# Products of 512 token columns issued as two products of 256 columns in one accumulation group

## The chip, the cores and the metric

The kernel runs on one core of a Trainium2 chip. The metric is device time in microseconds (us) for one execution of the whole program. TensorE (PE in the profile) multiplies, VectorE (DVE) and ScalarE (ACT) do the elementwise work and empty the accumulators, GpSimd (POOL) does a little elementwise work, and SyncE (SP) issues the transfers.

## The reference, cut to what matters

A two-layer backbone runs over 512 tokens: 256 context tokens, which form a prefix, and 256 latent tokens. The same weights serve both kinds.

```python
for layer in range(DEPTH):                       # 2 layers
    h_l = modulate(rmsnorm(lat, ...), ...)       # latent tokens
    h_c = modulate(rmsnorm(cx, ...), ...)        # context tokens
    ...
    if layer % 2 == 0:                           # layer 0: SSD + retention heads
        y_c, st = ssd_retention_mixer(h_c, None, ab_zero_states(b), *p)
        y_l, _ = ssd_retention_mixer(h_l, rope, st, *p)
    else:                                        # layer 1: mLSTM heads
        ...
    lat = block_update(lat, y_l, ...)            # residual, then the feed-forward network
    if layer < DEPTH - 1:
        cx = block_update(cx, y_c, ...)

def swiglu(h, w1, w3, w2):
    return (jax.nn.silu(h @ w1) * (h @ w3)) @ w2
```

Nearly all arithmetic is in the dense products: the input projection `ab_in_w` (1024 x 6160), the output projection `ab_out_w` (2048 x 1024), two feed-forward networks with 2816 hidden columns, and the mLSTM's `ml_up_w` (1024 x 4096) and `ml_down_w` (2048 x 1024). Everything is float32, and the kernel keeps that accuracy by splitting each operand into two parts (below).

## The kernel before, in words

**Layout.** Activations lie feature by token: 128 features on the partitions, tokens along the free dimension. Columns 0 to 255 are the context (`CT_`), columns 256 to 511 the latent tokens (`LT_`). So a product of one weight tile (128 x 128, stationary, loaded by a LDWEIGHTS before each matmul) with all tokens streams 512 columns and fills one accumulator tile of 128 x 512 float32, one bank of the accumulator memory.

**Split products.** Weights arrive as float32 (`wraw`), and ACT rounds each to fp32r (`wH`, L367) while DVE takes what is left (`wL`, L227). Activations are split the same way (`hH`, `hL` for the normalised input, `uH`, `uL` for the hidden layer of the feed-forward network, `yH`, `yL` for what enters the output projection). The helper `mm3` (L401 to L407) then issues three matmuls for each pair of a weight tile and an activation tile, wH with H, wH with L, wL with H, and adds them all up in one accumulation group. L405, L406 and L407 are these three. Every such matmul has a LDWEIGHTS of its own (PEld in the profile).

**Who calls `mm3` with how many columns.** With 512 columns: the four query and key tiles of the very first stage (`p4`, L591), the input projection's feature tiles (`projA`, L698), the output projection (`out_quarter`, L1038), and layer 0's feed-forward network (`ffn0`, L1144), which takes `projA` for its first product and its own loop for the second. With 256 columns: `projB` (L705), in which an activation tile is stationary and 256 weight columns stream; the last four output tiles before each norm (`tail_tiles`, L1002); the first tiles after it (`head_tiles`, L1022), which work on one half of a 512-column accumulator at a time; and all of layer 1, whose `projA` already works half by half (L701), since its activations are stored in halves (`packed`).

**Feed-forward network of layer 0.** The 22 hidden tiles come in three parts of 8, 8 and 6. In each part `projA` makes two tiles, `ffn_act` (L1131) turns them into one hidden tile (ACT: silu, DVE: `u`, ACT: `uH`, DVE: `uL`), and when all tiles of the part are there, the second product (called f2 here, L1162) accumulates over them, hidden tile after hidden tile, and DVE adds the result to the residual stream (`upd`, L974).

**Order.** A scheduler that is part of the framework orders the instructions of PE, ACT, DVE and POOL; SP's order is the program's. PE executes its matmuls in the order given, and one that waits for an operand holds up all behind it. There are four accumulator tiles for these products (`mmps`, tag "mm") and four buffers each for `wH` and `wL`.

Of the kernel before, what the change touches and what calls it, by code (L numbers as in the profile page):

```python
# [186 lines left out]
def tile_hybrid(ctx, tc, A, out, dbg=None):  # L187
# [16 lines left out]
    def s2(p="s2", shape=(P, 512), dt=F32):  # L204
        return sb.tile(list(shape), dt, tag="s2", name=nm(p), bufs=36)
# [25 lines left out]
    CT_, LT_, ALL = slice(0, 256), slice(256, 512), slice(0, 512)  # L231
# [169 lines left out]
    def mm3(o, pairs, first=True, last=True):  # L401

        n = len(pairs)
        for i, ((lh, ll), (rh, rl)) in enumerate(pairs):
            TE.matmul(o, lhsT=lh, rhs=rh, start=first and i == 0, stop=False)  # L405
            TE.matmul(o, lhsT=lh, rhs=rl, start=False, stop=False)  # L406
            TE.matmul(o, lhsT=ll, rhs=rh, start=False, stop=last and i == n - 1)  # L407
# [5 lines left out]
    def cols(hl, sl):  # L413
        return tuple(t[:, sl] for t in hl)
# [156 lines left out]
    for i, k in enumerate(seq):  # L571
        ld(i + 3)
        wload()
        if i < 4:
            if i > 0:
                wprep()
            w4.append(wready.pop(0))
        if i == 0:
            xn = h_a(k, rb, amix[0], ALL)
        h_b(hs[k], k, xn, mod[0][0], ALL)  # L580
        if i == 0:
            prep(1)
        prep(i + 2)
        TE.matmul(pdt[0:32, :], lhsT=wdt[:, k, :], rhs=hs[k](ALL)[0], start=i == 0, stop=False)
        TE.matmul(pdt[0:16, :], lhsT=wdt[:, k, 0:16], rhs=hs[k](ALL)[1], start=False, stop=i == KD - 1)
        if i + 1 < KD:
            fin(i + 1)
            xn = h_a(seq[i + 1], rb, amix[0], ALL)
        for j, w in enumerate(w4):
            for n in range(i + 1) if j == i else (i,):  # L590
                mm3(p4[j], [(wk(w, seq[n]), hs[seq[n]](ALL))], n == 0, n == KD - 1)  # L591
# [106 lines left out]
    def projA(hs):  # L698
        w = wnext()
        p = mmps()  # L700
        for sl in (CT_, LT_) if hs[0].packed else (ALL,):  # L701
            mm3(p[:, sl], [(wk(w, k), hs[k](sl)) for k in range(KD)])
        return p

    def projB(hs, evac):  # L705
        ws = [wnext(), wnext()]
        for c in range(NCH):
            p = mmps([P, 256])
            sl = slice(c * P, (c + 1) * P)
            mm3(p, [(hs[k](sl), tuple(ws[k // 4][z][:, (k % 4) * 256:(k % 4 + 1) * 256] for z in range(2)))  # L710
                    for k in range(KD)])
            evac(c, p)
            slot()
# [774 lines left out]
    for m in range(KD):  # L1488
        o = s2("fin")[:, :256]
# [22 lines left out]
```

## Time and profile before

| | |
|---|---|
| time, median of 3 runs | 1348.47 us (1346.25 to 1348.91) |
| the profiled execution, its own time | 1344.61 us |
| its span, from the first to the last instruction | 1342.8 us |
| TensorE busy | 1308.1 us (97%) |
| VectorE busy | 945.6 us (70%) |
| ScalarE busy | 643.2 us (48%) |
| mean granted TensorE clock | 0.988 of full speed |

Matmuls are pipelined: the profile gives each a duration from its start to a modelled end, and these overlap. A 512-column matmul is shown with some 0.39 us, though the next one starts 0.23 us after it. What a matmul costs in a stream is therefore the distance from start to start, and it is read from the times at which instructions start. A TensorE that is shown busy all the time may still stream faster or slower.

### The profile page before, as it was taken

To read this page: it belongs to the slowest core of one execution; us is meant where nothing else is said; L and a number is where in the kernel's file an instruction comes from. 1 tells how busy PE (TensorE), PEld (TensorE's weight loads), DVE (VectorE), ACT (ScalarE), POOL (GpSimd) and SP (SyncE) were. 2 spreads that over 40 slices of the span, in tenths; PEclk is the share of its full clock that TensorE was granted. 3 is DMA by queue.
4 is the path that set the end of the run, shared out by engine and by line. 5 is a ranking of instruction groups with operands and counts; after the bars stand their busy time and mean duration, and the time that the engine had idled before them with its cause. 6 is when DMAs were issued, how large, how long until landed. Compare 5 with 4: busy or idle time off the path is not lost.

```text
span 1342.8 us, 20999 instructions
## 1 busy us (share of the span) xinstructions
PE 1308.1 (97%) x8158; PEld 1147.5 (85%) x8158; DVE 945.6 (70%) x1703; ACT 643.2 (48%) x1114; POOL 124.8 (9%) x138
## 2 busy tenths in 40 slices
PE   7999999999999999999999999989999999999997
PEld 3699888988899898888888888989999689999997
DVE  7888797966865578797557634586666897666555
ACT  4465757836763243222222233466556563544443
POOL 0022032211021030000000210300000000000001
PEclk9999999999999999999999999999999999899998
DMA  9337344434312225566547622411124334365553
GB/s 367 112 144 235 122 163 155 133 117 161 117 64 87 94 79 204 179 213 236 195 170 248 240 94 94 140 66 63 48 69 144 134 109 142 130 206 199 191 196 118
DMA packets 60837, 200.70 MB, mean 149 GB/s; under 512 B 6841, under 2 KB 8377, under 8 KB 60737
## 3 DMA queue, kind: packets, MB, share of 16 engines
q1 hardware_dynamic: 60594, 199.36, 43.0%
q8 instruction: 64, 1.05, 0.3%
q14 instruction: 35, 0.29, 0.1%
q10 hardware_dynamic: 144, 0.01, 0.0%
HBM read 197.16 MB, written 1.13 MB: 148 GB/s over the span
## 4 chain that ended last, share of the span: by engine, by line
PE 82%; DVE 7%; issue 4%; DMA 2%; ACT 2%; POOL 1%; SPq 0%; POOLq 0%; DVEq 0%; ACTq 0%
PE mm L405 24%; PE mm L406 24%; PE mm L407 24%; DVE wL L227 2%; PE sc L954 2%; PE mm L1215 1%; ACT wH L367 1%; PE sc L836 1%; DVE junk L291 1%; DMA ada<-in_ada 1%; DMA wraw<-in_wup 1%; PE sc L841 1%; PE sc L818 1%; DVE junk L267 1%; PE sc L732 1%
## 5 line engine op out<-in xcount | busy, mean ns | idle before, releaser
L367 ACT CAST wH<-wraw 128x1024 fp32r<-128x1024 f32 x248 | 259.4, 1048 | 415.1 <-PE mm L406 298.1
L227 DVE TENSOR_TENSOR wL<-wraw,wH 128x1024 fp32r<-128x1024 f32 x248 | 305.1, 1232 | 139.6 <-ACT wH L367 129.7
L406 PE MATMUL mm<-hL,wH 128*128 128x512 f32 (+1 forms) x568 | 219.7, 387 | 0.4 <-DVE hL L496 0.4
L407 PE MATMUL mm<-hH,wL 128*128 128x512 f32 (+1 forms) x568 | 219.4, 387 | 0.0
L405 PE MATMUL mm<-hH,wH 128*128 128x512 f32 (+1 forms) x568 | 217.7, 390 | 1.5 <-ACT wH L367 1.5
L267 DVE SCALAR_TENSOR_TENSOR junk<-ada,cbc 128x1024 bf16<-128x1024 f32 x128 | 157.9, 1233 | 19.6 <-DMA ada<-in_ada 18.1
L405 PEld LDWEIGHTS mm<-hH,wH 128*128 128x128 f32 x568 | 107.0, 190 | 25.8 <-ACT wH L367 2.0
L406 PEld LDWEIGHTS mm<-hL,wH 128*128 128x128 f32 x568 | 107.7, 190 | 24.4 <-DVE hL L496 0.6
L407 PEld LDWEIGHTS mm<-hH,wL 128*128 128x128 f32 x568 | 107.6, 189 | 23.7
L405 PE MATMUL mm<-wH,hH 128*128 128x256 f32 x384 | 110.4, 288 | 0.0
L979 DVE SCALAR_TENSOR_TENSOR xt<-mm,mod,xt 128x256 f32<-128x256 f32 x144 | 64.4, 479 | 63.8 <-PE mm L407 63.5
L406 PE MATMUL mm<-wL,hH 128*128 128x256 f32 x384 | 107.9, 281 | 0.0
L407 PE MATMUL mm<-wH,hL 128*128 128x256 f32 x384 | 107.4, 280 | 0.0
L405 PE MATMUL mm<-hp,wH 128*128 128x256 f32 x384 | 107.3, 284 | 0.1
L406 PE MATMUL mm<-hp,wH 128*128 128x256 f32 x384 | 106.9, 281 | 0.0
L683 DVE SCALAR_TENSOR_TENSOR conv<-xp,prm,conv 128x512 f32<-128x512 f32 x128 | 96.5, 757 | 14.8 <-ACT conv L680 13.8
L407 PE MATMUL mm<-hp,wL 128*128 128x256 f32 x384 | 106.7, 280 | 0.0
L405 PE MATMUL mm<-hHL,wH 128*128 128x256 f32 x352 | 97.6, 279 | 1.1 <-ACT hHL L495 1.1
L406 PE MATMUL mm<-hHL,wH 128*128 128x256 f32 x352 | 97.7, 278 | 0.0
L407 PE MATMUL mm<-hHL,wL 128*128 128x256 f32 x352 | 97.7, 278 | 0.0
L405 PEld LDWEIGHTS mm<-hp,wH 128*128 128x128 f32 x384 | 72.6, 191 | 2.7 <-ACT conv L680 1.1
L405 PE MATMUL mm<-uH,wH 128*128 128x512 f32 (+1 forms) x200 | 73.6, 368 | 0.0
(329 smaller groups left out, 2876.2 us busy)
## 6 DMA issues: line engine op xcount, KB each, us to landing
wraw<-in_f SPq DMA_DIRECT2D x136, 512.0 KB, 4.0
ada<-in_ada SPq DMA_DIRECT2D x80, 512.0 KB, 4.6
wraw<-in_win SPq DMA_DIRECT2D x48, 512.0 KB, 4.4
wraw<-in_wup SPq DMA_DIRECT2D x32, 512.0 KB, 3.3
erow<-scr SPq DMA_DIRECT2D x16, 512.0 KB, 6.8
wraw<-in_wout SPq DMA_DIRECT2D x16, 512.0 KB, 3.7
wraw<-in_wdn SPq DMA_DIRECT2D x16, 512.0 KB, 3.3
adaf<-in_ada SPq DMA_DIRECT2D x10, 512.0 KB, 8.0
```

Of the source, the lines that this page charges most:

```text
L227: eng.tensor_tensor(out=o, in0=a, in1=b, op=op)
L267: V.scalar_tensor_tensor(out=junk, in0=raw, scalar=1.0, in1=cbc[:, st, :], op0=ALU.mult, op1=ALU.mult, accum_out=mod[l][c][:, k, st:st + 1])
L291: V.scalar_tensor_tensor(out=junk, in0=raw, scalar=1.0, in1=cbc[:, st, :], op0=ALU.mult, op1=ALU.mult, accum_out=to)
L367: S.copy(out=H, in_=raw)
L405: TE.matmul(o, lhsT=lh, rhs=rh, start=first and i == 0, stop=False)
L406: TE.matmul(o, lhsT=lh, rhs=rl, start=False, stop=False)
L407: TE.matmul(o, lhsT=ll, rhs=rh, start=False, stop=last and i == n - 1)
L683: V.scalar_tensor_tensor(out=o, in0=x[:, :, k:k + 256], scalar=pc(wname, t * 5 + k), in1=o, op0=ALU.mult, op1=ALU.add)
L732: TE.transpose(p[:, c * P:(c + 1) * P], tiles[:, c, f * P:(f + 1) * P], ident)
L818: TE.matmul(p[:, d, :], lhsT=btok[:, c, :], rhs=vws[n][:, d, :], start=True, stop=True)
L954: TE.matmul(py[:, i, :], lhsT=src[:, i * P:(i + 1) * P], rhs=vt[:, j, :], start=j == 0, stop=j == len(srcs) - 1)
L979: V.scalar_tensor_tensor(out=xt[:, m, half], in0=p[:, o:o + 256], scalar=gate[:, m, st:st + 1], in1=xt[:, m, half], op0=ALU.mult, op1=ALU.add)
```

## The change

`mm3` looks at the width of its output. Over 256 columns it now calls itself twice, for the context half and then for the latent half of the same accumulator tile. The first call opens the accumulation group, the second closes it. Each of the two goes through all pairs of its list, so that the weight tiles are loaded once more for the second half.

```diff
     def mm3(o, pairs, first=True, last=True):
 
         n = len(pairs)
+        if o.shape[-1] > 256:
+            for sl in (CT_, LT_):
+                mm3(o[:, sl], [(lp, cols(rp, sl)) for lp, rp in pairs], first and sl is CT_, last and sl is LT_)
+            return
         for i, ((lh, ll), (rh, rl)) in enumerate(pairs):
             TE.matmul(o, lhsT=lh, rhs=rh, start=first and i == 0, stop=False)
             TE.matmul(o, lhsT=lh, rhs=rl, start=False, stop=False)
             TE.matmul(o, lhsT=ll, rhs=rh, start=False, stop=last and i == n - 1)
```

The four new lines move the three matmuls to L409, L410 and L411.

Two places on TensorE show what this does to its order. Names are the tiles' with a running number; the halves of a tile are not told apart in them. The first place is in layer 0's feed-forward network, where one `projA` tile ends and the next begins. Before:

```order
L405 MATMUL mm_5109<-hH_4689,wH_4862 128x512
L406 MATMUL mm_5109<-hL_4690,wH_4862 128x512
L407 MATMUL mm_5109<-hH_4689,wL_4863 128x512
L405 MATMUL mm_5159<-hH_4675,wH_5097 128x512
L406 MATMUL mm_5159<-hL_4676,wH_5097 128x512
L407 MATMUL mm_5159<-hH_4675,wL_5098 128x512
```

With the change, inside the second of these tiles (now `mm_6095`), where the context half ends and the latent half begins:

```order
L409 MATMUL mm_6095<-hH_5601,wH_6009 128x256
L410 MATMUL mm_6095<-hL_5602,wH_6009 128x256
L411 MATMUL mm_6095<-hH_5601,wL_6010 128x256
L409 MATMUL mm_6095<-hH_5587,wH_6009 128x256
L410 MATMUL mm_6095<-hL_5588,wH_6009 128x256
L411 MATMUL mm_6095<-hH_5587,wL_6010 128x256
```

The eight activation tiles are gone through twice, with 24 matmuls of 256 columns each time, where there were 24 of 512 columns.

The second place is the start of f2 in the first part of that network, where the last hidden tile (`uH_5624`, `uL_5625` before, `uH_6848`, `uL_6849` with the change) is used for the first time. Before:

```order
L405 MATMUL mm_5649<-uH_5540,wH_5559 128x512
L406 MATMUL mm_5649<-uL_5541,wH_5559 128x512
L407 MATMUL mm_5649<-uH_5540,wL_5560 128x512
L405 MATMUL mm_5649<-uH_5624,wH_5559 128x512
L406 MATMUL mm_5649<-uL_5625,wH_5559 128x512
L407 MATMUL mm_5649<-uH_5624,wL_5560 128x512
```

With the change:

```order
L409 MATMUL mm_6873<-uH_6716,wH_6735 128x256
L410 MATMUL mm_6873<-uL_6717,wH_6735 128x256
L411 MATMUL mm_6873<-uH_6716,wL_6736 128x256
L409 MATMUL mm_6873<-uH_6848,wH_6735 128x256
L409 MATMUL mm_6937<-uH_5999,wH_6790 128x256
L410 MATMUL mm_6937<-uL_6000,wH_6790 128x256
L410 MATMUL mm_6873<-uL_6849,wH_6735 128x256
L411 MATMUL mm_6873<-uH_6848,wL_6736 128x256
L409 MATMUL mm_6873<-uH_5999,wH_6735 128x256
```

Before, 21 matmuls of 512 columns stand between the start of f2 and the first use of the last hidden tile. Now 21 of 256 columns stand there, and the scheduler puts two matmuls of the next output tile (`mm_6937`) between the use of `uH_6848` and that of `uL_6849`, which is thus the 25th matmul of f2. The latent half follows. The second part has the same order. In the third, with six hidden tiles, 16 matmuls and then 8 of the next tile stand ahead of the last `uL`: 24 again. The transfers that SP issues, and POOL's instructions, are the same in the same order; on ACT and DVE some neighbours change places.

## Rows read from the trace of the kernel before

**Rows 1.** The page: span, and busy time, share, and instructions of engines.
```profile
span 1342.8 us, 20999 instructions
...
PE 1308.1 (97%) x8158; PEld 1147.5 (85%) x8158; DVE 945.6 (70%) x1703; ACT 643.2 (48%) x1114; POOL 124.8 (9%) x138
```

**Rows 2.** Busy time in stretches: first tiles; layer 0's mixer; its feed-forward network.
```profile
core 0: us, PE busy (x) PEld busy (x) DVE busy (x) ACT busy (x) POOL busy (x), PEclk, DMA share, GB/s
0.00:60.00 60.00, 49.47 (x176) 28.13 (x177) 50.17 (x129) 22.54 (x43) 1.22 (x5) 0.97 0.67 259
60.00:493.00 433.00, 429.55 (x2633) 383.25 (x2632) 323.33 (x556) 262.45 (x490) 84.78 (x91) 0.99 0.40 130
493.00:845.00 352.00, 352.00 (x1575) 286.77 (x1574) 232.76 (x373) 98.04 (x125) 17.35 (x18) 1.00 0.51 181
```

**Rows 3.** Who waited for whom: us in total, times, longest.
```profile
PE mm L405 <- ACT xcH L1196: 4.4, 1, 4.4
...
ACT wH L367 <- PE mm L406: 298.1, 118, 4.6
```

**Rows 4.** Instruction groups by shape: 512-column matmuls of L406, all three kinds.
```profile
L406 PE MATMUL mm<-hL,wH 128*128 128x512 f32 x520 | 206.0, 396 | 0.0
...
L406 PE MATMUL mm<-uL,wH 128*128 128x512 f32 x152 | 60.1, 396 | 0.0
...
L406 PE MATMUL mm<-yL,wH 128*128 128x512 f32 x112 | 44.2, 395 | 0.0
```

**Rows 5.** Timeline of PE, f2's first part (start us, us): first matmul, first behind.
```profile
582.00 0.39 PE L405 MATMUL mm<-uH,wH 128*128 128x512 f32 x1
...
626.80 0.39 PE L405 MATMUL mm<-hH,wH 128*128 128x512 f32 x1
```

**Rows 6.** PE busy (x matmuls), clock, DMA: layer 1's feed-forward network, only 256-column matmuls.
```profile
1154.20:1331.80 177.60, 177.60 (x1569) 1.00 0.53 181
```

**Rows 7.** Timeline of PE, a `projB` in layer 0: first and last of 96 matmuls.
```profile
331.67 0.28 PE L405 MATMUL mm<-wH,hH 128*128 128x256 f32 x1
...
342.86 0.28 PE L407 MATMUL mm<-wH,hL 128*128 128x256 f32 x1
```

**Rows 8.** Timeline of PE, a later `projB` in layer 0: first and last of 47.
```profile
418.94 0.28 PE L406 MATMUL mm<-wL,hH 128*128 128x256 f32 x1
...
424.16 0.28 PE L407 MATMUL mm<-wH,hL 128*128 128x256 f32 x1
```

**Rows 9.** Timeline of PE, `head_tiles` of the network: first and last of 105 matmuls.
```profile
497.30 0.28 PE L407 MATMUL mm<-hH,wL 128*128 128x256 f32 x1
...
509.09 0.28 PE L407 MATMUL mm<-hH,wL 128*128 128x256 f32 x1
```

**Rows 10.** Instruction groups, weight loads: for 512 (48 for 256) columns, and for 256.
```profile
L406 PEld LDWEIGHTS mm<-hL,wH 128*128 128x128 f32 x568 | 107.7, 190 | 24.4 <-DVE hL L496 0.6 <-issue 0.3
...
L406 PEld LDWEIGHTS mm<-hp,wH 128*128 128x128 f32 x384 | 72.8, 190 | 0.8 <-issue 0.2
```

**Rows 11.** Timeline, f2's second part: start, last `uL`, a modulation multiplication, `uL`'s use.
```profile
716.40 0.39 PE L405 MATMUL mm<-uH,wH 128*128 128x512 f32 x1
...
718.63 0.68 DVE L227 TENSOR_TENSOR uL<-u,uH 128x512 fp32r<-128x512 f32 x1
719.23 1.22 DVE L267 SCALAR_TENSOR_TENSOR junk<-ada,cbc 128x1024 bf16<-128x1024 f32 x1
...
721.53 0.39 PE L406 MATMUL mm<-uL,wH 128*128 128x512 f32 x1
```

**Rows 12.** Timeline, last quarter of the output projection: first two matmuls, `yL` made.
```profile
450.51 0.47 PE L405 MATMUL mm<-yH,wH 128*128 128x512 f32 x1
450.82 0.40 PE L406 MATMUL mm<-yL,wH 128*128 128x512 f32 x1
...
450.97 1.29 DVE L227 TENSOR_TENSOR yL<-sc,yH 128x512 fp32r<-128x512 f32 x2 [0.18 <-ACT yH L720]
```

## The prediction, made before the changed kernel ran

> **What bounds the kernel now.** I read the page first: TensorE is shown busy 97% of the span, DVE 70%, ACT 48% [rows 1]. Then the stretches. PE is idle for 10.5 of the first 60 us, for 3.5 of the 433 us of layer 0's mixer, and never in the 352 us of its feed-forward network [rows 2]. The view of waits says the same from both sides: the longest that PE waits for one thing is 4.4 us, while ACT, which prepares the weights, waits 298.1 us for PE to give back a `wH` buffer [rows 3]. So from 60 us on the time is the number of matmuls by their distance from start to start, and the other engines have time left. All 512-column products lie ahead of 845 us. The prediction rests on one question: how far apart are two 256-column matmuls, against one of 512 columns?
>
> **How many.** The groups by shape have 520, 152 and 112 matmuls of 512 columns for L406 [rows 4], 784 in all, and L405 and L407 have as many: 2352 matmuls become 4704. In the feed-forward network it is 41 `projA` tiles of 24 matmuls, two f2 parts of 8 tiles by 24 and one of 4 tiles by 18: 984 + 384 + 72 = 1440. The other 912 are in the mixer and the first stage.
>
> **Distance at 512 columns.** f2's first part has 8 x 24 = 192 matmuls from 582.00 to 626.80 us [rows 5]: 44.80 / 192 = 233.3 ns. Other stretches read alike.
>
> **Distance at 256 columns.** It has two values. Layer 1's feed-forward network runs 1569 such matmuls in 177.60 us without one interruption [rows 6]: 113.2 ns, and its timeline, from first to last, 113.3. A `projB` in layer 0 has 96 of them from 331.67 to 342.86 us, 11.19 / 95 = 117.8 ns [rows 7]; a later one has 47 in 5.22 us, 5.22 / 46 = 113.5 [rows 8]. I call them the short and the long distance. A stretch keeps the one that it begins with: none of those of 40 and more matmuls has both, except where the first dozen are slower. It changes where other matmuls (transposes, the scans' products) come between. Of the 13 such stretches ahead of 437 us 4 have the short one, with 236 matmuls, and 9 the long one, with 612.
>
> So the pair costs 2 x 113.3 = 226.6 ns, 6.7 less than the one that it replaces, or 2 x 117.8 = 235.6, 2.3 more. Which of them the new stream gets decides the sign.
>
> **The change, part by part.**
>
> The weight loads double. A load is recorded with 190 ns, in the groups of 512 columns and in one of 256 alike [rows 10], so it lies beside other matmuls in either case: 113 ns from start to start have room for it. The distances above include it, so it costs nothing more.
>
> Feed-forward network of layer 0: 1440 matmuls. The stream in front of it, `head_tiles`, already has the form that the change makes everywhere: 256-column slices of the 512-column `hH` and `hL`, written to one half of an accumulator. It has 105 matmuls in 11.79 us, 11.79 / 104 = 113.4 ns [rows 9], the short distance. Nothing but these products runs on PE from there to 845 us, as in layer 1's network, which kept the short one to its end. I take the short distance: 1440 x 6.7 = **-9.6 us**. At the long one it would be 1440 x 2.3 = +3.3.
>
> Mixer and first stage: 912 matmuls, cut up by the scans' matmuls. I take the mix of the 13 stretches, 28% short: 2 x (0.28 x 113.3 + 0.72 x 117.8) = 233.1 ns, **-0.2 us**. The bounds are -6.1 (all short) and +2.1 (all long). The first stage's products wait for DVE anyway.
>
> A new wait, at the start of each part of f2. The last `projA` tile still has to go through ACT and DVE. In the second part f2 begins at 716.40 us, and the last `uL` is there at 718.63 + 0.68 = 719.31, 2.91 us later. Before, it was first used at 721.53, with 2.2 us to spare [rows 11]. With the change its first use is the 25th matmul of 256 columns, 24 x 0.1133 = 2.72 us after the start. All behind it on PE wait for 0.2 us. The other two parts read 2.92 and 2.91 us, and have 24 matmuls ahead too: 3 x 0.2 = **+0.6 us**. It can be nothing, if the chain is quicker by that, or 1.2 us more each, if one DVE multiplication of the modulation stands in front of `u` (one of these takes 1.22 us [rows 11]).
>
> The same in the last quarter of the output projection. Its first tile starts at 450.51 us and its second matmul at 450.82; the two last `yL` are made from 450.97 to 452.26 [rows 12], the first of them at some 451.6. Their first uses would be 6 and 9 matmuls after 450.82, at 451.5 and 451.84: waits of 0.1 and, after that, 0.3 us: **+0.4 us**.
>
> Transfers and POOL keep their order. DVE has 232.8 us of work in the network's 352 us [rows 2], 66%; at 3% less time per tile this is 68%: room enough.
>
> Sum: -9.6 - 0.2 + 0.6 + 0.4 = **-8.8 us**. The profiled execution took 1344.6 us (span 1342.8 and 1.8 around it), so the changed kernel's would take 1335.8. The median of the runs shown is 3.9 us above the profiled one; from it, 1348.5 - 8.8 = **1339.7 us**.
>
> **A rule against the change.** The rows show that the part of the distance which is not columns is not the same for both: at 2.4 GHz, which the granted clock of 1.00 in [rows 6] stands for, 512 columns take 213.3 ns and leave 20.0 of 233.3, 256 take 106.7 and leave 6.6 of 113.3. The Trainium skill, page "TensorE: Matmul & The Clock Gate", section "Back-to-back issue gap", has a fixed part instead: 262 cycles for 256 columns, 518 for 512. By it, as an estimate, each pair would cost 6 cycles or 2.5 ns more, 2352 x 2.5 = +5.9 us for the kernel. The rows agree neither with 518 cycles (215.8 ns) nor, at the short distance, with a split that costs; but a stream at the long distance would behave as the rule says, and it is the second rival.
>
> **The rivals.**
>
> First, only a part of the stream stays short. A wait inside a stream of 256-column matmuls, without other matmuls and without a lower clock, is nowhere in the rows, so each of the new waits might begin the stream anew at the long distance. If this takes the 576 matmuls from the first f2 to the second, or the 480 behind, half of the network's gain goes: 528 x 9.0 (6.7 lost and 2.3 added) = 4.8 us, which leaves -4.0: 1344.5 us.
>
> Second, the other side: the new stream runs at the long distance, in the network from the first f2 at the latest. 312 matmuls stay short (-2.1), 1128 cost 2.3 more (+2.6), the mixer +2.1 at its worst and the waits +0.8: 1351.9 us; with the network long from its start as well +3.3 + 2.1 + 0.8 = +6.2, 1354.7. For it speaks that 9 of 13 stretches in the mixer are long; against it that both networks' streams, each of which follows a norm, begin short [rows 6, 9]. The sum is positive as soon as fewer than 30% of the 2352 are short: -6.7 a + 2.3 (1 - a) + 0.4 = 0 for a = 0.30, with 0.4 ns each for the waits.
>
> Third, another engine takes the gain: weights, hidden tiles or transfers come no earlier, and PE waits for what it saves. The 298.1 us that ACT waits for PE [rows 3] speak against it. It would give 1348.5.
>
> Fourth, the weight loads lie bare after all, as they would if a second load of 190 ns could not start under a matmul of 256 columns: 2352 x (2 x 190 - 233.3) = +345 us, 1693 us. The 113.2 ns of [rows 6] all but exclude it.
>
> **How the numbers follow.** The forecast has 0.50, the first rival 0.20, the second 0.18, the third 0.11, the fourth 0.01. The forecast alone reaches from -14.7 (the mixer all short, as above) to -5: 1333.8 to 1343.5. For 8 in 10 the range takes in the first and third rivals and the near end of the second: 1333.5 to 1350.5 us. 0.2% are 2.7 us, about what a measurement of this kernel can tell from no change. Faster by more: the forecast and the first rival, 0.70. Within it: the third and some of the second, 0.15. Slower by more: the rest of the second, the fourth, 0.15.
>
> **What would show it.** In the changed profile: 4704 more rows of 256 columns, none of 512 on the three lines; distances of 113.3 ns through the network (its 352 us become some 343); three waits of PE on `uL` of some 0.2 us; the stretch from 60 to 493 us unchanged within 2 us; layer 1 the same. Distances of 117.8 in the network, or waits of a microsecond and more at f2, would make it wrong.

## The result, and the profile after

The changed kernel takes **1342.44 us** (median of 20 runs, 1334.51 to 1350.77), the kernel before 1348.69 us beside it (20 runs, 1345.77 to 1355.96). The ratio is 0.9946, with a 95% interval of 0.9930 to 0.9961: 5.3 to 9.4 us less, where 8.8 were forecast. Of all runs in this document one, of 1356.27 us in experiment 2, counts as slow; it stands in that kernel's median and is left out of its ratio. The profiled execution took 1343.85 us. It is only 0.76 us below the profiled one of before, and this is the first thing to explain.

The page of the changed kernel, its first lines and one group of its matmuls:

```profile
span 1341.9 us, 25691 instructions
...
PE 1305.2 (97%) x10510; PEld 1250.5 (93%) x10510; DVE 947.8 (71%) x1703; ACT 642.1 (48%) x1114; POOL 125.0 (9%) x138
...
L410 PE MATMUL mm<-hL,wH 128*128 128x256 f32 x1088 | 303.1, 279 | 0.7 <-DVE hL L500 0.7
```

There are 2352 more matmuls and as many more weight loads than in [rows 1], and no group of 512 columns is left on the three lines of `mm3`, which are now L409, L410 and L411 (x1088 are the 2 x 520 of [rows 4] and 48 that had 256 columns before). PE's share is again 97%: it does not tell how fast the stream runs. What does move is PEld, the weight loads: 85% before, 93% now.

The same stretches as in [rows 2], with layer 1's network below them (columns as there):

```profile
0.00:60.00 60.00, 50.44 (x261) 33.94 (x262) 50.13 (x129) 22.43 (x43) 1.22 (x5) 0.97 0.67 260
60.00:493.00 433.00, 427.01 (x3455) 416.88 (x3455) 324.69 (x555) 261.61 (x489) 83.95 (x91) 0.99 0.40 130
493.00:845.00 352.00, 350.65 (x3039) 349.84 (x3038) 235.39 (x377) 99.37 (x128) 18.51 (x20) 1.00 0.54 183
1154.05:1331.55 177.50, 177.50 (x1568) 177.50 (x1567) 106.37 (x135) 84.08 (x118) 5.16 (x5) 1.00 0.56 181
```

In the network of layer 0 PE was never idle before; now it is for 1.35 us of the 352. The mixer has lost 2.5 us more to idle time (433.00 - 427.01 against 3.45). In the view of waits, ACT still waits longest for PE, with 236.3 us in the row that answers to the 298.1 of [rows 3]:

```profile
ACT wH L367 <- PE mm L410: 236.3, 105, 4.6
```

The timeline of PE (start us, us). First the matmuls of the two norms around the network in the kernel before, then, in the changed kernel, the same two and between them the matmuls around the waits at the starts of f2:

```profile
482.86 0.50 PE L423 MATMUL sc<-ones,acc 128*128 128x1 f32 x4
...
855.41 0.50 PE L423 MATMUL sc<-ones,acc 128*128 128x1 f32 x4
```

```profile
483.61 0.50 PE L427 MATMUL sc<-ones,acc 128*128 128x1 f32 x4
...
582.75 0.28 PE L411 MATMUL mm<-uH,wL 128*128 128x256 f32 x1
583.64 0.50 PE L409 MATMUL mm<-uH,wH 128*128 128x256 f32 x2 [0.61 <-ACT uH L1144]
...
584.73 0.39 PE L410 MATMUL mm<-uL,wH 128*128 128x256 f32 x1 [0.47 <-DVE uL L227]
584.95 0.28 PE L411 MATMUL mm<-uH,wL 128*128 128x256 f32 x1
...
715.30 0.28 PE L410 MATMUL mm<-uL,wH 128*128 128x256 f32 x1
715.78 0.38 PE L410 MATMUL mm<-uL,wH 128*128 128x256 f32 x1 [0.21 <-DVE uL L227]
716.00 0.28 PE L411 MATMUL mm<-uH,wL 128*128 128x256 f32 x1
...
827.89 0.48 PE L409 MATMUL mm<-uH,wH 128*128 128x256 f32 x2
...
829.44 0.28 PE L411 MATMUL mm<-uH,wL 128*128 128x256 f32 x1
...
853.15 0.50 PE L427 MATMUL sc<-ones,acc 128*128 128x1 f32 x4
```

The idle time in brackets is not all that a wait costs, since a matmul that is shown as still running hides a part of it. From start to start, the 5 distances from 582.75 to 584.95 us take 2.20 us where 0.57 would do at 113.3 ns, the 2 from 715.30 to 716.00 us 0.70 for 0.23, and the 10 from 827.89 to 829.44 us 1.55 for 1.13. The three places cost 1.6, 0.5 and 0.4 us, 2.5 in all, of which 1.35 us are shown as idle.

And the network's four long streams as windows, from the start of the first matmul of each to the start of its last (one or two of the PE count overlap the edges):

```profile
498.88:582.75 83.87, 83.87 (x742) 83.87 (x741) 68.85 (x115) 28.73 (x40) 0.00 (x0) 1.00 0.52 184
587.91:714.96 127.05, 127.05 (x1124) 127.05 (x1122) 86.40 (x140) 33.47 (x40) 0.00 (x0) 1.00 0.62 211
719.07:827.78 108.71, 108.71 (x926) 108.71 (x924) 56.62 (x84) 27.95 (x35) 14.50 (x16) 1.00 0.49 161
831.73:853.04 21.31, 21.31 (x191) 21.31 (x189) 10.26 (x16) 8.12 (x12) 7.38 (x6) 1.00 0.30 100
```

The first is 83.87 / 740 = 113.3 ns from start to start, the second 127.05 / 1121 = 113.3, the third 108.71 / 923 = **117.8**, the fourth 113.4. Between the second and the third stands the wait of 0.21 us at 715.78: behind it the stream began anew at the long distance and kept it until f2's third part began, at 827.89 us; behind that place it is short again. The granted clock is 1.00 in all four, so the clock is not what sets the distance.

From norm to norm the network went from 372.55 us (482.86 to 855.41 before) to 369.54, 3.0 less. The parts give nearly that: -9.6 for 1440 pairs at the short distance, +4.3 for the 948 matmuls of the third stream at 4.5 ns each, +2.5 for the three places. Besides, the mixer ended 0.75 us later, and what lies behind, which the change does not touch, took 1.4 us longer, 1341.9 - 853.15 against 1342.8 - 855.41. Together that is the 0.9 us between the spans.

### The profile page after: what moved, and what is told of

It is laid out like the page before. It is cut to its first block, busy times and chain, and to the rows that moved or that the text cites. A ratio compares the mean times of both kernels' runs of the same rounds, so it can differ in the third digit from the quotient of the medians.

```text
span 1341.9 us, 25691 instructions
## 1 busy us (share of the span) xinstructions
PE 1305.2 (97%) x10510; PEld 1250.5 (93%) x10510; DVE 947.8 (71%) x1703; ACT 642.1 (48%) x1114; POOL 125.0 (9%) x138
## 3 DMA queue, kind: packets, MB, share of 16 engines
HBM read 197.16 MB, written 1.13 MB: 148 GB/s over the span
## 4 chain that ended last, share of the span: by engine, by line
PE 69%; DVE 13%; issue 7%; DMA 5%; ACT 3%; POOL 1%; SPq 0%; POOLq 0%; DVEq 0%; ACTq 0%
PE mm L410 20%; PE mm L409 20%; PE mm L411 20%; DVE wL L227 3%; DVE junk L267 3%; DMA ada<-in_ada 2%; PE sc L958 1%; ACT wH L367 1%; DMA erow<-scr 1%; PE mm L1219 1%; DVE junk L291 1%; PE sc L840 1%; DVE conv L687 1%; DVE comb L227 1%; DMA wraw<-in_wup 1%
## 5 line engine op out<-in xcount | busy, mean ns | idle before, releaser
L367 ACT CAST wH<-wraw 128x1024 fp32r<-128x1024 f32 x248 | 259.4, 1048 | 408.0 <-PE mm L410 236.3
L410 PE MATMUL mm<-hL,wH 128*128 128x256 f32 x1088 | 303.1, 279 | 0.7 <-DVE hL L500 0.7
L409 PE MATMUL mm<-hH,wH 128*128 128x256 f32 x1088 | 299.5, 279 | 2.8 <-ACT hH L499 2.1
L411 PE MATMUL mm<-hH,wL 128*128 128x256 f32 x1088 | 301.8, 279 | 0.0
L409 PEld LDWEIGHTS mm<-hH,wH 128*128 128x128 f32 x1088 | 204.3, 190 | 4.5 <-ACT hH L499 2.8
L410 PEld LDWEIGHTS mm<-hL,wH 128*128 128x128 f32 x1088 | 205.7, 189 | 2.0 <-DVE hL L500 1.7
L411 PEld LDWEIGHTS mm<-hH,wL 128*128 128x128 f32 x1088 | 205.5, 189 | 0.5
L409 PE MATMUL mm<-wH,hH 128*128 128x256 f32 x384 | 110.2, 287 | 0.2 <-ACT conv L684 0.2
L409 PE MATMUL mm<-hp,wH 128*128 128x256 f32 x384 | 108.6, 287 | 0.1
L410 PE MATMUL mm<-hp,wH 128*128 128x256 f32 x384 | 108.2, 284 | 0.0
L410 PE MATMUL mm<-wL,hH 128*128 128x256 f32 x384 | 108.0, 282 | 0.1
L411 PE MATMUL mm<-hp,wL 128*128 128x256 f32 x384 | 108.1, 283 | 0.0
L411 PE MATMUL mm<-wH,hL 128*128 128x256 f32 x384 | 107.4, 280 | 0.0
L410 PE MATMUL mm<-uL,wH 128*128 128x256 f32 x352 | 98.2, 279 | 0.7 <-DVE uL L227 0.7
L409 PE MATMUL mm<-hHL,wH 128*128 128x256 f32 x352 | 97.6, 279 | 1.1 <-ACT hHL L499 1.1
L409 PE MATMUL mm<-uH,wH 128*128 128x256 f32 x352 | 97.8, 279 | 0.6 <-ACT uH L1144 0.6
L410 PE MATMUL mm<-hHL,wH 128*128 128x256 f32 x352 | 97.8, 278 | 0.0
L411 PE MATMUL mm<-hHL,wL 128*128 128x256 f32 x352 | 97.8, 278 | 0.0
```

What stands on the lines that cost most here:

```text
L367: S.copy(out=H, in_=raw)
```

## The experiments

**The theory** that they test: a stream of 256-column matmuls runs at one of two distances, 113.3 or 117.8 ns; which one is decided by what PE did just ahead of it, and at a wait it can come out differently from one execution to the next (the expectations say "drawn"). Rivals: the waits cost what they are shown with and no more; or the gain is in every split product alike.

Medians in us, ratios to the kernel before on the same chip; "high" counts the runs of 1343.5 us and more, which for most of these kernels, though not for the split in the network alone and the change again, lie apart from the others:

| kernel | median | ratio, 95% interval | high |
|---|---|---|---|
| halves in turn | 1341.34 | 0.9943, 0.9912 to 0.9974 | 6 of 12 |
| covered second product | 1335.28 | 0.9904, 0.9873 to 0.9935 | 4 of 12 |
| the same again | 1341.19 | 0.9929, 0.9894 to 0.9965 | 3 of 9 |
| split in the network alone | 1342.76 | 0.9959, 0.9935 to 0.9984 | 5 of 12 |
| split in mixer and first stage alone | 1348.53 | 0.9991, 0.9966 to 1.0016 | - |
| the change again | 1339.03 | 0.9927, 0.9901 to 0.9954 | 2 of 7 |
| covered, 4 matmuls of 128 columns ahead | 1338.31 | 0.9933, 0.9906 to 0.9960 | 3 of 12 |
| covered, 4 matmuls of 1 column ahead | 1356.90 | 1.0050, 1.0034 to 1.0066 | 12 of 12 |
| covered, block of 16 ahead | 1336.46 | 0.9905, 0.9872 to 0.9937 | 1 of 9 |
| the same again | 1338.09 | 0.9905, 0.9873 to 0.9936 | 0 of 6 |
| before, 4 matmuls of 128 columns ahead of layer 1's network | 1350.93 | 1.0012, 0.9994 to 1.0030 | - |

**1. Halves in turn.** Each weight tile meets the context half and then the latent half, so that no f2 part has its last operand earlier than before.

```diff
         if o.shape[-1] > 256:
-            for sl in (CT_, LT_):
-                mm3(o[:, sl], [(lp, cols(rp, sl)) for lp, rp in pairs], first and sl is CT_, last and sl is LT_)
+            for i, (lp, rp) in enumerate(pairs):
+                for sl in (CT_, LT_):
+                    mm3(o[:, sl], [(lp, cols(rp, sl))], first and i == 0 and sl is CT_, last and i == n - 1 and sl is LT_)
```

> The same 4704 matmuls of 256 columns, but context half and latent half follow each other for each pair of tiles, so that the last hidden tile is first used after 42 of them (4.8 us) and not after 24 (2.7 us). Theory (the distance from start to start is drawn anew at every wait): no wait of PE on the hidden tiles in the feed-forward network of layer 0, one stream at 113.3 ns from its first tiles to its last, 9 us less than before in this network, 1339 us by the median of before of 1348.7, and less spread between runs than the 16 us of the changed kernel. Rival (only the waits themselves cost, 1.3 us in all, the spread has another source): 1341 us, with the same spread. Second rival (two loads of the same weights on end change the distance): another distance than 113.3 or 117.8 ns in the trace.

The network in the profiled execution (1350.93 us): the two norms around it, and one window from its head tiles to its end:

```profile
484.10 0.50 PE L428 MATMUL sc<-ones,acc 128*128 128x1 f32 x4
...
860.66 0.50 PE L428 MATMUL sc<-ones,acc 128*128 128x1 f32 x4
```

```profile
498.73:860.54 361.81, 361.81 (x3074) 361.81 (x3073) 231.16 (x370) 99.05 (x129) 22.00 (x22) 1.00 0.54 179
```

No wait is left in it, and it is one stream of 3073 matmuls, long from start to end: 361.81 / 3072 = 117.8 ns. The runs do not lie closer together, as I expected, but in two groups of six, 1334.87 to 1339.17 and 1343.5 to 1353.15. This fits a distance that is drawn once for the whole network where no wait stands inside, instead of once for each part; in the unprofiled runs the streams themselves are not seen.

**2. Covered second product.** Only f2's first two tiles are issued in another way: both run over all hidden tiles but the last, and then the last for both, so that ACT and DVE have the time of 84 matmuls for it, some 9.5 us, where they had that of 24 with the plain change and of 21 of 512 columns (4.9 us) before.

```diff
...
+            ws2 = [wnext() for _ in range(2)]
+            ps2 = [mmps() for _ in ws2]
+            for w, p in zip(ws2, ps2):
+                mm3(p, [(wk(w, k), us[k]) for k in range(nk - 1)], True, False)
+            for w, p in zip(ws2, ps2):
+                mm3(p, [(wk(w, nk - 1), us[nk - 1])], False, True)
...
```

> The changed kernel, with one edit in layer 0's feed-forward network: each second product begins with two output tiles over all hidden tiles but the last, and then takes the last one for both, so that 84 matmuls of 256 columns (9.5 us; 60 and 6.8 us in the third part) stand ahead of its first use. Theory: as for the halves taken in turn, no wait and one stream at 113.3 ns through the network, 1339 us, less spread. Rival: 1341 us and the spread of the changed kernel.

The norms around layer 0's network, and the two networks as windows (profiled execution of 1332.07 us):

```profile
480.83 0.50 PE L427 MATMUL sc<-ones,acc 128*128 128x1 f32 x4
...
843.66 0.50 PE L427 MATMUL sc<-ones,acc 128*128 128x1 f32 x4
```

```profile
496.18:843.54 347.36, 347.36 (x3067) 347.36 (x3066) 228.97 (x368) 98.30 (x128) 21.97 (x22) 1.00 0.54 186
1141.54:1319.19 177.65, 177.65 (x1568) 177.65 (x1568) 106.60 (x136) 84.30 (x118) 5.18 (x5) 1.00 0.59 181
```

Here 3066 matmuls take 347.36 us, 113.3 ns each. The window above has seven more; for equal counts the difference is 3065 x 4.5 ns, or **13.7 us**, at the same granted clock, with the same DMA share of 0.54 and with PE busy throughout in both. The order of the matmuls differs between the two kernels; experiments 5 and 6 have the same pair of distances at one order. Repeated beside later kernels it had 3 of 9 high runs:

> The kernel with the covered second product once more, unchanged, beside the block. By both theories 1331 to 1338 us where both networks are short; by the theory that the distance is drawn at each start, some of the runs again at 1344 to 1357 us (4 of 12 before), by a rival that puts the first session's slow group down to the chip of that session, none.

The profiled execution of that repeat (1339.64 us) shows layer 0's network short and layer 1's, which no kernel here changes, long: 183.16 us for 1557 matmuls, 117.7 ns each, 5.5 us more than above for 11 matmuls fewer:

```profile
496.36:843.73 347.37, 347.37 (x3068) 347.37 (x3066) 230.07 (x369) 98.58 (x129) 22.13 (x22) 1.00 0.54 186
1144.25:1327.41 183.16, 183.16 (x1557) 183.16 (x1557) 104.90 (x131) 83.47 (x116) 5.15 (x5) 1.00 0.58 176
```

This repeat ran on another chip than the first twelve runs, and the high runs are there again: they do not belong to one chip.

**3. Where the gain is.** A flag in `mm3` turns the split on at the head of the network (`halves[0] = True`) or off there.

> The split only in layer 0's feed-forward network (1440 of the 2352 matmuls), the mixer and the first stage as before. Theory: the mixer's part of the change is worth nothing (233.1 against 233.3 ns a pair, with 0.4 us and more of new waits), so this is at the changed kernel's time or 1 us under it, 1341 to 1342 us, with the waits at the second products still there. Rival (the mixer carries part of the gain): 1345 us or more.

> The split in the first stage and the mixer alone (912 matmuls of 512 columns become 1824); both networks as before. The prediction's mixer term was -0.2 us, the profile of the changed kernel had its mixer end 0.75 us later: 1348 to 1350 us, within 0.2% of before, by the theory that the gain lies in the network of layer 0. A rival that sees the gain in every split product (912 x 2 x 3.35 ns = 6.1 us where all were short) expects 1342 to 1344 us.

The network alone gives 0.9959, mixer and first stage alone 0.9991; their product, 0.9950, is close to the whole change (0.9946). The rival that sees the full gain in every split product, 1342 to 1344 us for the mixer, is out: 6.1 us less lie outside the interval, which ends at 4.6. A smaller gain in the mixer is not excluded by it. In the profiled execution of the split in the network alone (1353.36 us) it is the second of the windows that is long, and layer 1's network too:

```profile
584.77:590.30 5.53, 5.07 (x28) 4.86 (x29) 4.79 (x9) 0.00 (x0) 0.00 (x0) 0.69 0.71 233
590.65:722.68 132.03, 132.03 (x1123) 132.03 (x1122) 86.59 (x139) 33.32 (x40) 0.00 (x0) 1.00 0.58 201
726.60:831.21 104.61, 104.61 (x925) 104.61 (x924) 55.18 (x84) 27.89 (x35) 14.19 (x16) 1.00 0.51 167
1156.84:1340.86 184.02, 184.02 (x1563) 184.02 (x1563) 105.73 (x133) 83.87 (x117) 5.15 (x5) 1.00 0.55 175
```

The first line is the stretch ahead of the long stream. PE had waited 2.31 us for `uH` just before it and waits 0.46 us for `uL` in it. The granted clock is 0.69 there, and 15 of its distances are 213 ns, which is 256 columns at 1.2 GHz. From 582.18 to 590.42 us 29 distances take 8.23 us instead of 3.29: in this execution the new wait alone cost 4.9 us, which is half of what the split gains in the network. Whether the long distance behind it comes from the wait or from the change of clock is not told apart.

**4. The change again, unchanged.**

> The changed kernel once more, for a second profiled execution. Theory: 1342 us with runs from 1335 to 1351; in the profile the waits at the second products of layer 0's feed-forward network are there again, of 0.2 to 1 us, but which stretches behind them run at 113.3 and which at 117.8 ns differs from the first profile, and so do those of layer 1, which the change does not touch. Rival (the distance is fixed by the program): the same stretches at the same distances as in the first profile.

The second and third of the four windows, as above:

```profile
585.68:712.73 127.05, 127.05 (x1124) 127.05 (x1122) 86.39 (x140) 33.45 (x40) 0.00 (x0) 1.00 0.63 211
716.73:821.34 104.61, 104.61 (x925) 104.61 (x924) 55.57 (x84) 27.89 (x35) 14.58 (x16) 1.00 0.52 168
```

The third part, 108.71 us in the first profile, is 104.61 here, in the same program behind the same wait of 0.21 us. So at this place the order of the instructions does not fix the distance: it comes out only when the program runs.

That does not hold everywhere. Between 110 and 484 us, in the mixer, the ten profiled executions that have the split there show 23 stretches of 40 and more such matmuls. In 18 of them the distance is the same in all ten executions, short in some and long in others; five come out one way or the other. Nor does a stretch need a wait to change. This is one stretch of 503 matmuls of the changed kernel, without a gap, in two windows:

```profile
298.84:344.99 46.15, 46.15 (x410) 46.15 (x408) 33.48 (x47) 28.20 (x53) 5.84 (x8) 1.00 0.50 161
344.99:356.18 11.19, 11.19 (x98) 11.19 (x96) 8.26 (x12) 9.84 (x16) 0.00 (x0) 1.00 0.28 92
```

The first has 407 distances of 113.4 ns, the second 95 of 117.8. At 344.99 us a `projB`, in which the weights stream, ends and a `projA`, in which the activations stream, begins. In all eight executions in which this stretch was short up to there it changed at this matmul; in the other two it was long throughout. The network has no such place, since only activations stream in it.

**5. What is ahead of a stream.** A few matmuls into an accumulator tile that nobody reads, in the covered kernel, behind the head tiles of both networks; first 4 of 128 columns, then 4 of one column. These are additional work; nothing is left out.

```diff
...
+    def settle(h):
+        p = scps([P, NCH, P])
+        for c in range(NCH):
+            TE.matmul(p[:, c, 0:1], lhsT=f32v(h), rhs=ones[:, 0:1], start=True, stop=True)
...
+        settle(h2[KD - 1](LT_)[0][:, 0:P])
...
```

> The kernel of the second experiment (split, and two output tiles at the start of each second product) with four float32 matmuls of 128 columns added once behind the first tiles of each of the two feed-forward networks; their result is not used. In the profiles so far every stream of 256-column products that came straight behind four such matmuls (those of the SSD scores) had the short distance, 16 of 16, whatever stood before. Theory (a stream takes its distance from what stands in front of it, and a wait or a change of clock leaves it to chance): both networks run at 113.3 ns in every execution, the slow group of runs (4 of 12, at 1344 us and more) is gone, all runs at 1332 to 1338 us plus 1 to 2 us for the eight added matmuls. Rival (the distance has another cause, such as where in time the execution starts): two groups of runs as in the second experiment, 8 to 14 us apart.

> The same kernel, but the four added float32 matmuls have one column each. In the profiles so far every stream behind four such matmuls (the sums of squares for a norm) had the long distance, 12 of 12. Theory: both networks run at 117.8 ns in every execution: 3066 and 1568 matmuls by 4.5 ns, 14 and 7 us more than with the added matmuls of 128 columns, one group of runs at 1352 to 1358 us. Rival (another cause): two groups of runs, most of them at 1332 to 1338 us.

With the one-column matmuls all 12 runs are high, in one group, 1352.52 to 1359.39. Their median is 20.9 us above the middle of the nine low runs with 128 columns on the same chip (1335.96); (2959 + 1510) x 4.5 ns are 20.1. The profile of that kernel, head tiles ahead of the four matmuls, the stream behind them, and the one behind the four in layer 1:

```profile
494.45:506.56 12.11, 12.11 (x107) 11.98 (x106) 8.17 (x21) 5.36 (x11) 0.00 (x0) 1.00 0.01 2
507.69:856.07 348.38, 348.38 (x2959) 348.38 (x2959) 221.83 (x350) 92.42 (x117) 21.73 (x22) 1.00 0.54 186
1162.59:1340.31 177.72, 177.72 (x1510) 177.72 (x1510) 104.40 (x131) 81.77 (x115) 5.17 (x5) 1.00 0.58 181
```

The head tiles are at the short distance but for one break of some 0.2 us; the stream behind is at 348.38 / 2958 = 117.8 ns for all of 348 us. The mirror image failed: 4 matmuls of 128 columns did not keep the high runs away, 3 of 12 were left. In the kernel before, ahead of layer 1's network, they changed nothing either:

> The kernel before, without the split, with the four added float32 matmuls of 128 columns behind the first tiles of layer 1's feed-forward network alone. Its 512-column products have one distance, so its spread should come from layer 1's network. Theory: the runs of before at 1355 to 1358 us (4 of 30) are gone, the median stays within 1 us of before, 1348 to 1350 us. Rival: the spread of before, with a few runs at 1355 us and more.

Its ratio of 1.0012 has an interval on both sides of 1, and runs of 1354.02 to 1357.81 us were still there. Four matmuls of that kind are not what makes a stream short.

**6. A longer block.** In the profiles all streams behind one place of the SSD scan were short: 20 of 20 when this was planned, 40 of 40 in the ten executions with the split in the mixer. What stands there is 12 transposes and 4 matmuls of 128 columns; this block was put in front of both networks. By itself the 40 of 40 says little of the block, since 18 of 23 stretches of the mixer have one distance in every execution.

```diff
...
+        for i in range(12):
+            TE.transpose(p[:, i % 4, :], f32v(h), ident)
+        for i in range(4):
+            TE.matmul(p[:, i, :], lhsT=f32v(h), rhs=cst[:, 0:128], start=True, stop=True)
...
```

> The kernel with the covered second product, plus a block of 12 transposes (128x128) and 4 matmuls of 128 columns behind the head tiles of both networks, into a tile that nobody reads: the same kinds and number of PE work that stand ahead of each stream of the SSD scan that was short in 20 of 20 streams. If what stands ahead of a stream sets its distance (113.3 or 117.8 ns), both networks' main streams are short in every execution: one group of runs, at 1332 to 1340 us, none above 1344. If the distance is drawn by chance at a wait, whatever work stands ahead, 3 or 4 of 12 runs lie at 1344 to 1357 us, as with 4 matmuls of 128 columns alone.

> The kernel with the block of 12 transposes and 4 matmuls of 128 columns once more, unchanged: 8 of its 9 runs lay at 1333.7 to 1339.7 us, one at 1351.2. If the block makes the streams behind it short, at most one of the new runs lies above 1344 us; if the distance is still drawn by chance, about a third do, as with the covered second product alone (7 of 21).

Together 1 of 15 runs is high, against 7 of 21 for the covered kernel without the block. Both profiled executions happen to show the step itself. In the first it is in layer 1: head tiles, and the stream behind the block:

```profile
1145.42:1150.61 5.19, 5.19 (x46) 5.19 (x45) 0.00 (x0) 0.47 (x1) 0.00 (x0) 1.00 0.01 3
1153.06:1324.08 171.02, 171.02 (x1511) 171.02 (x1510) 103.71 (x130) 80.77 (x113) 5.17 (x5) 1.00 0.62 188
```

In the second it is in layer 0: head tiles, the stream behind the block, and then layer 1's stream:

```profile
497.43:509.80 12.37, 12.37 (x108) 12.37 (x106) 6.99 (x18) 4.70 (x10) 0.00 (x0) 1.00 0.01 2
512.25:847.49 335.24, 335.24 (x2961) 335.24 (x2959) 221.47 (x348) 91.41 (x116) 22.22 (x22) 1.00 0.56 193
1157.05:1328.08 171.03, 171.03 (x1511) 171.03 (x1510) 103.66 (x130) 80.73 (x113) 5.17 (x5) 1.00 0.61 188
```

The head tiles are long (5.19 / 44 and 12.37 / 105, 118.0 and 117.8 ns), and the streams behind the block are short (171.02 / 1509 and 335.24 / 2958, 113.3 both). So behind the block a long stream went on as a short one in two of two cases, as behind the one-column matmuls a short one went on as a long one in two of two. That it always does is not shown: one run of 15 was at 1351.2 us, without a profile, and 1 of 15 against 7 of 21 may still be chance. It is not told apart either whether the block does it or any interruption of that length.

**7. Other sizes.** Two products of 384 and 128 columns instead of two halves; one run.

```diff
...
+            for sl in (slice(0, 384), slice(384, 512)):
...
```

> Every product of 512 columns issued as one of 384 and one of 128 columns, the same count of matmuls and loads as with halves. It tells the distance by the number of columns. If the part that is not columns (20 ns at 512, 6.6 or 11.1 at 256) grows with the columns, 384 columns take some 160 + 13 = 173 ns; if it is a step at 512, 167 to 171. 128 columns take 53 ns alone, and between 60 and 113 ns if the weight load sets the distance. Theory of the load: a stream of 128-column matmuls stands some 107 to 113 ns apart, so that the pair costs 270 to 285 ns, 37 to 52 more than 233.3, and the kernel 85 to 120 us more. Rival (loads lie wholly beside other matmuls): 230 ns a pair and no change of the time.

It took 1503.8 us, 155 more than before, above the expected. In its timeline of PE the 128-column part of a tile and the 384-column part follow each other:

```profile
599.76 0.28 PE L411 MATMUL mm<-hH,wL 128*128 128x128 f32 x1
...
601.43 0.27 PE L411 MATMUL mm<-hH,wL 128*128 128x128 f32 x1
...
601.77 0.34 PE L410 MATMUL mm<-hL,wH 128*128 128x384 f32 x1
...
603.72 0.34 PE L409 MATMUL mm<-hH,wH 128*128 128x384 f32 x1
...
669.36 0.69 PE L409 MATMUL mm<-uH,wH 128*128 128x384 f32 x1 [8.53 <-ACT uH L1144]
```

15 distances of 128 columns are 1.67 us, **111.3 ns** each; 11 of 384 are 1.95 us, 177.3 ns. A pair costs 288.6 instead of 233.3, and 2352 x 55.3 ns = 130 us. The rest is not in these distances: waits for the hidden tile at the start of f2 parts, 8.53 us here (DVE stood 4.90 us at a modulation multiplication that waited for its transfer, ahead of the hidden tile's own), 3.0 us at the next part, and a granted clock of 0.83 in the 31 us behind the longest.

## Why the prediction was right, point by point

**The count and the two distances** hold: 4704 matmuls, at 113.3 or 117.8 ns and nothing between.

**The network, -9.6 at the short distance, +3.3 at the long one.** Both ends were seen, from norm to norm (372.55 us before): 362.83 with the covered f2 and all short, -9.7; 376.56 with the halves in turn and all long, +4.0. What failed is the sentence that a stream keeps the distance that it begins with. The rows on which it rested [rows 6, 7, 8] are one execution, and none of them has a wait inside or a change from streaming weights to streaming activations. Behind a wait the distance can be another, at the change of roles it can be too, and at the same wait it differs between executions of the same program. The first rival was priced for this, -4.0 in all for a part of the stream, with a chance of 0.20. In the profile after it is what happened: 948 of the network's matmuls long, 948 x 4.5 ns = 4.3 us lost of the 9.6. In the second profiled execution of the same kernel nothing in the network was long.

**The new waits, +0.6 at three f2 starts.** They came to 2.5 us from start to start: 1.6, 0.5 and 0.4 in the profile after, and 1.7, 0.5 and 0.5 in the second execution. The term was too small mainly for two reasons. It took only the time by which the last `uL` comes late, while the matmul behind each wait also stands some 0.22 us from the next one, where 0.113 is the rule (584.73 to 584.95, 715.78 to 716.00). And the first place is the dear case that the prediction named, a multiplication of the modulation in front of `u`; a weight split of 1.22 us stands in front of `uL` too. DVE in the changed kernel:

```profile
580.90 1.23 DVE L267 SCALAR_TENSOR_TENSOR junk<-ada,cbc 128x1024 bf16<-128x1024 f32 x1
...
582.25 0.69 DVE L227 TENSOR_TENSOR u<-u,mm 128x512 f32<-128x512 f32 x1
582.86 1.22 DVE L227 TENSOR_TENSOR wL<-wraw,wH 128x1024 fp32r<-128x1024 f32 x1
583.99 0.68 DVE L227 TENSOR_TENSOR uL<-u,uH 128x512 fp32r<-128x512 f32 x1
```

Besides, each is a place where the distance can change, worth 4.3 us in the profile after. The covered f2 has none of them, and its best run took 1331.71 us.

**The mixer, -0.2.** In the profiled pair it ended 0.75 us later, with waits that I had not foreseen: 0.64 us for ACT's `zs` at 229.28 us, 0.77 for DVE's `vw` at 248.29. They also stand, at 0.42 to 0.71 and 0.76 to 0.80, in eight other profiled executions with the halves one after the other. The kernel that splits there alone came out at 0.9991, with an interval of 0.9966 to 1.0016: between 4.6 us less and 2.2 more. The profiles measure it better, and the profile after is the least favourable of them. From the first matmul of the first norm to that of the norm ahead of the network, the nine executions with the halves one after the other took 467.6 to 470.9 us, in the middle 468.7; the three without the split took 470.0, 471.4 and 472.9. By the middle values the mixer gained 2.7 us, and the term was too small. The step that failed is the mix: the 13 stretches were all `projB` products, in which the weights stream. The products that the change splits stream activations, and 59 to 75% of their matmuls were short in these nine executions, where the sum took 28%. At 71%, as in the profile after, a pair costs 229.2 ns, and 912 of them -3.7 us, less the new waits.

**The output projection, +0.4.** In the profile after no such wait stands in its last quarter: from 452.44 us on its matmuls are 113.3 ns apart. The term was wrong, and too small to be seen in the time.

**The sum, -8.8.** It came near the measured 5.3 to 9.4 us less in part by luck. With what was measured, and the network all short, it would be -9.6 + 2.5 - 2.7 = -9.8: the waits came out 1.9 us dearer, the mixer with the output projection 2.9 us cheaper, and the two nearly cancel. What is still missing to the measured gain fits the long streams of some executions (4.3 us in the profile after), which the sum had at nothing.

**The weight loads at nothing.** At 256 columns they do stay hidden at the short distance. But the margin is thin: PEld is busy all through these windows, as PE is, and at 128 columns the distance falls no lower than 111.3 ns. By that number, as an estimate, a split in four would take 4 x 111.3 = 445 ns, nearly twice the 233.3; it was not run.

The Trainium skill, page "TensorE: Matmul & The Clock Gate", section "LDWEIGHTS (loading the stationary operand)", gives a load the time of its columns at 1.2 GHz, 106.7 ns for 128 as an estimate. The 111.3 ns measured at 128 columns are 4% above that; whether the load is what sets this distance was not tried.

**The rule against the change.** With 128, 256, 384 and 512 columns the distances are 111.3, 113.3 (or 117.8), 177.3 and 233.3 ns. What is left above the columns at 2.4 GHz (53.3, 106.7, 160.0, 213.3) is 58.0, 6.6 (or 11.1), 17.3 and 20.0: no fixed part. 256 is the size at which the two come closest, and this is why a split into halves gains and the uneven one does not.

**The second rival** (the whole stream long, 1351.9 to 1354.7 us) did not decide the median, but it is real: the profile of the halves in turn has the whole network long, 6 of its 12 runs are high, and the one-column matmuls put every run at 1352.5 to 1359.4. **The third** (another engine takes the gain) is out: ACT still waits 236.3 us for PE.

**Profiled run and median.** The 3.9 us between them, which I had only added, stay without a shown cause. Layer 1's network takes 177.6 us short and 183 to 184 long, in kernels that leave it as it is, and the profile of before had it short. That may be what the 5 of 20 runs of before at 1352.3 us and more are, though none of them was profiled. But the median of before lies with the other 15, at 1345.8 to 1349.8.

## What to carry to other kernels

In a dense stream read the distance from start to start at the sizes that the kernel already has before choosing a column count: here two of 256 columns at the short distance come out 6.7 ns cheaper than one of 512, and one of 128 is nearly as dear as one of 256. Read it in products that stream the same operand, and count a wait from start to start and not by the idle time alone. When an accumulation is reordered, look at when its last operand is first needed; cover it with a second output tile, and the profiled streams have neither the wait nor a change of distance at it. That the covered kernel is faster than the plain change is not shown: 0.9904 and 0.9929 against 0.9946 and 0.9927, with intervals that overlap, and the same holds for the covered kernel with the block ahead, 0.9905 twice. And when a profile shows one execution, ask which of its streams could have come out otherwise, before a row of it is multiplied by a thousand.

## What the runs showed of the hardware that was not expected

Two streams of the same 2959 matmuls in the same order, one behind four matmuls of one column and one behind the block, take 348.38 and 335.24 us at the same granted clock of 1.00 and at DMA shares of 0.54 and 0.56, and PE and the weight loads show as busy throughout in both. The distance can hold for hundreds of microseconds. It can change at a wait, and also without one, where the streamed operand changes from weights to activations. At most places of the mixer (18 of 23) it is the same in every execution; at the network's start and its waits it is not. It can be pushed: behind four matmuls of one column all 12 runs had the long time, and both networks were long in the one that was profiled. Behind a block of 12 transposes and 4 matmuls 14 of 15 runs had the short one, against 14 of 21 without the block, which may still be chance. What in the array or in its queue is in one of two states has not been found.
